# A spatial gate's mean taken by a centering product on TensorE, and a gelu with its addition folded in

## The chip, the cores and the metric

One core of one Trainium2 chip runs the kernel. The metric is the device time of one execution in microseconds (us), the median of the runs. The engines are TensorE (PE, its weight loads PEld), VectorE (DVE), ScalarE (ACT), GpSimd (POOL) and SyncE (SP), which issues the transfers.

## What is computed

One layer of a gated two-branch block on x (1024 tokens, width 1024), all in float32: a norm, one combined projection into nine parts, an attention branch (eight heads of 64), a spatial-gating branch, two merge gates, an output projection, a residual and a last norm. What the change touches is the spatial gate's v branch and the gelu in front of it:

```python
def spatial_gating(u, v, ln_g, ln_b, w_s, b_s):
    b, s, g, c = v.shape                       # 8 groups of 64 channels
    mu = jnp.mean(vf, axis=-1, keepdims=True)
    var = jnp.mean(jnp.square(vf - mu), axis=-1, keepdims=True)
    vn = (vf - mu) * lax.rsqrt(var + EPS) * ln_g + ln_b
    ...
    mixed = jnp.einsum('gts,bnsgc->bntgc', w, vn) + b_s ...
    return u * mixed

y_b = spatial_gating(jax.nn.gelu(u_b), jax.nn.gelu(v_b), ...) * jax.nn.silu(z_b)
```

The gelu is computed in its sigmoid form, v * sigmoid(1.5957691 * v * (1 + 0.044715 * v * v)).

## The kernel before

Every float32 product is made of three passes over operands that are split into a high and a low part (type fp32r): high by high, high by low, low by high. ScalarE casts the high part, VectorE or GpSimd subtracts it to get the low one (`hi_lo`, lines 214 to 216). The combined projection is done in groups of two 128-channel tiles by 1024 tokens; `project` (line 528) makes one group with seven products of twelve passes each (a Strassen scheme), and hands each finished 128 x 512 quarter to a function `use`. So each branch gets its data in quarters, channels on the partitions and tokens along the free axis.

No engine's order is written by hand. All operations are first recorded as tasks with an estimated cost (`Plan.add`, line 104); a list scheduler (`issue`, line 234) then plays them through on five engines and the transfer queue and issues them in the order that comes out. On each engine the ready task with the lowest priority number goes first. The number is the place in the program, less an offset: parts called through `ahead` (line 813) get 6000 off and the weights' preparation 9000, on every engine but TensorE. TensorE itself takes the earliest ready task of the program. A task starts only if its buffers are free, and buffers of one tag are granted in the order of the program: the tags "tr" and "z" have two PSUM banks each, "o", "X", "Y" and "Z" one, the small columns "s" sixteen buffers (line 353). At run time each engine works its list in order.

The sections come in this order (lines 827 to 854): the norm of x and the attention's values, then the first groups of keys and queries, u, the second gate path, v (`make_vb(0)`) and the attention's gate, the first attention head, then u, gate path and v of the second half (`make_vb(1)`) ahead of their turn, and the other heads with the remaining projections between them. In the trace the eight units of `make_vb` lie in 140 to 200 us and 250 to 306 us.

One unit of `make_vb` (lines 768 to 810) takes a quarter v, 128 channels (two groups of 64) by 512 tokens:

- `gelu_gate` (line 714): a square on ScalarE, an addition with a scale on ScalarE (`act_add`, line 149), a multiplication on VectorE, a sigmoid on ScalarE; then a multiplication by v.
- four transposes on TensorE into one "tr" bank (line 777), which put tokens on the partitions and channels along the free axis.
- a sum over each group's 64 channels (line 780), and the subtraction of sum / 64, out of PSUM into SBUF (line 781), both on VectorE.
- a square on ScalarE, a sum on VectorE, an addition and a power on GpSimd (`rms_scale`, line 395), a multiplication by the resulting scale on VectorE (line 787).
- the split into high and low parts, six passes with the spatial weights into "o", a copy by ScalarE, four transposes back into a "z" bank, scale and shift on VectorE, and a multiplication by u and the gate path on GpSimd, with a transfer in and one out.

The u branch uses `gelu_gate` too, in eight quarters.

Of the kernel before, what the change touches and what calls it, by code (L numbers as in the profile page):

```python
# [10 lines left out]
F32 = mybir.dt.float32  # L11
F32R = mybir.dt.float32r
AF = mybir.ActivationFunctionType
ALU = mybir.AluOpType
AX = mybir.AxisListType

P = 128
# [4 lines left out]
GELU_C = 0.044715  # L22
GELU_S = 1.5957691216057308
# [66 lines left out]
class Plan:  # L90
# [10 lines left out]
    def buf(self, tag, shape=(P, 512), dt=F32):  # L101
        return Buf(self, tag, shape, dt)
# [22 lines left out]


    def mm(self, out, lhsT, rhs, start, stop, **kw):
        self.add("PE", max(0.109, rhs.n * 0.000417 + 0.0135),
                 lambda: self.nc.tensor.matmul(out.ap(), lhsT=lhsT.ap(), rhs=rhs.ap(), start=start, stop=stop, **kw),  # L129
                 [out], [lhsT, rhs])  # L130

# [198 lines left out]
def hybrid_block(  # L330
# [15 lines left out]
    nc = tc.nc  # L346
# [3 lines left out]
    dram = ctx.enter_context(tc.tile_pool(name="dram", bufs=1, space=bass.MemoryType.DRAM))  # L350
    ps = ctx.enter_context(tc.tile_pool(name="ps", bufs=1, space=bass.MemoryType.PSUM))

    slots = {"T": 14, "k": 6, "r": 5, "ak": 4, "e": 4, "f1": 4, "f2": 6, "a": 7, "b": 8, "os": 2, "s": 16,
             "X": 1, "Y": 1, "Z": 1, "z": 2, "tr": 2, "o": 1}
    psum_tags = {"X", "Y", "Z", "z", "tr", "o"}
    uid = [0]
# [11 lines left out]
    pl = Plan(tc, make_tile, slots, psum_tags)  # L368
    buf = pl.buf

    def cbuf(shape):
        return buf("c", shape)

    ident = cbuf((P, P))
    make_identity(nc, ident.ap())
    ident = ident.all
    nhalf = cbuf((P, 16))
    nc.vector.memset(nhalf.ap(), -0.5)
    one = cbuf((P, 16))
    nc.vector.memset(one.ap(), 1.0)  # L380
    sums = cbuf((P, 16))
    gcol = cbuf((P, 16))
    shift = cbuf((P, 4, P))
# [2 lines left out]
    def small(c=1):  # L386
        return buf("s", (P, 16))[:, 0:c]

    def blocks(v, k):
        return v.map(lambda a: a.rearrange("p (k c) -> p k c", k=k))  # L390

    def half_of(half):
        return slice(half * 512, half * 512 + 512)

    def rms_scale(ss_in, cols):
        ms = small(cols)
        pl.ts(ms, ss_in, EPS, None, ALU.add, eng="POOL")
        r = small(cols)
        pl.rsqrt(r, ms, nhalf[:, 0:cols])
        return r  # L400
# [116 lines left out]
    T = {1: hq[0, 0], 2: hq[1, 0], 3: hq[1, 1]}  # L517
# [10 lines left out]
    def project(g, use, keep=True):  # L528

        use_at, pl.offset = pl.offset, -9000  # L530

        def after(j, half, v, in_psum):
            pl.offset = use_at
            use(j, half, v, in_psum)
            pl.offset = -9000

        raw = {}
        for q in ((0, 0), (1, 0), (1, 1), (0, 1)):
            raw[q] = buf("a", (P, 4, P))
            pl.load(raw[q].all, w_pairs[g, 2 * q[0] + q[1]].rearrange("p (k e) -> p k e", e=P))  # L540

        def parts(v, eng="DVE"):
            hi, lo = buf("b", (P, 4, P), F32R), buf("b", (P, 4, P), F32R)
            pl.hi_lo(hi.all, lo.all, v.all, eng)
            return hi, lo

        def product(i, w, acc, start, stop=True):
            n = 0
            for kt in range(4):
                for a, b in ((w[0], T[i][0]), (w[0], T[i][1]), (w[1], T[i][0])):  # L550
                    pl.mm(acc.all, a[:, kt, :], b[:, kt, :], start and n == 0, stop and n == 11,
                          skip_group_check=True)
                    n += 1

        groups[0] += 1
        y, z, xx = buf("XY"[groups[0] % 2]), buf("Z"), buf("YX"[groups[0] % 2])
        s1 = s2 = s4 = buf("a", (P, 4, P))
        w1 = parts(raw[0, 0])
        pl.tt(s1.all, raw[1, 0].all, raw[1, 1].all, ALU.add, eng="POOL")
        w5 = parts(s1)  # L560
        product(1, w1, y, True)
        pl.copy(xx.all, y.all)
        pl.tt(s2.all, s1.all, raw[0, 0].all, ALU.subtract)
        product(5, w5, z, True)
        p5 = buf("f2")
        pl.copy(p5.all, z.all)
        w6 = parts(s2)
        product(6, w6, y, False)
        u2 = buf("f2")
        pl.copy(u2.all, y.all)  # L570
        w2 = parts(raw[0, 1], "POOL")
        s3 = raw[1, 0]
        pl.tt(s3.all, raw[0, 0].all, raw[1, 0].all, ALU.subtract, eng="POOL")
        product(2, w2, xx, False)
        after(0, 0, xx.all, True)
        w7 = parts(s3)
        product(7, w7, y, False)
        pl.tt(p5.all, y.all, p5.all, ALU.add)
        after(1, 1, p5.all, False)
        pl.tt(s4.all, raw[0, 1].all, s2.all, ALU.subtract)  # L580
        w3 = parts(s4)
        product(3, w3, z, False)
        pl.tt(u2.all, z.all, u2.all, ALU.add)
        after(0, 1, u2.all, False)
        w4 = parts(raw[1, 1], "POOL")
        product(4, w4, y, False)
        if keep:
            c21 = buf("f2")
            pl.copy(c21.all, y.all)
            after(1, 0, c21.all, False)  # L590
        else:
            after(1, 0, y.all, True)
        pl.offset = use_at
# [4 lines left out]
    def near(in_psum):  # L598
        return "DVE" if in_psum else "POOL"
# [114 lines left out]
    def gelu_gate(v, tag="f1"):  # L714
        t = buf(tag)
        pl.act(t.all, v, AF.Square)
        pl.act_add(t.all, t.all, one[:, 0:1], GELU_C)
        pl.tt(t.all, t.all, v, ALU.mult)
        pl.act(t.all, t.all, AF.Sigmoid, scale=GELU_S)
        return t  # L720

    uz = [buf("d", (P, S)) for _ in range(4)]
# [10 lines left out]
    def make_zb(a):  # L733
        def use(j, half, v, in_psum):
            t = buf("f1")
            pl.act(t.all, v, AF.Sigmoid)
            pl.tt(t.all, t.all, v, ALU.mult, eng=near(in_psum))
            us = buf("f1")
            pl.load(us.all, u[2 * a + j][:, half_of(half)])
            pl.tt(us.all, us.all, t.all, ALU.mult, eng="POOL")  # L740
            pl.store(uz[2 * a + j][:, half_of(half)], us.all)
        project(ZB[a], use)

    def wide(v):
        return v.map(lambda a: a.unsqueeze(2).broadcast_to([P, 8, 64]))
# [19 lines left out]
    def make_vb(a):  # L765
        ws = {}

        def use(j, half, v, in_psum):
            e = 2 * a + j
            if j not in ws:  # L770
                ws[j] = mix_weights(e)
                make_shift(e, ws[j])
            t = gelu_gate(v, "r")
            pl.tt(t.all, t.all, v, ALU.mult, eng=near(in_psum))
            tr = buf("tr")
            for n in range(4):
                pl.transpose(tr[:, n * P:(n + 1) * P], t[:, n * P:(n + 1) * P], ident)
            t3 = blocks(t.all, 8)
            mu = small(8)
            pl.reduce(mu, blocks(tr.all, 8))  # L780
            pl.stt(t3, wide(mu), -1.0 / 64, blocks(tr.all, 8), ALU.mult, ALU.add)
            sq = buf("f1")
            pl.act(sq.all, t.all, AF.Square, scale=0.125)
            vs = small(8)
            pl.reduce(vs, blocks(sq.all, 8))
            r = rms_scale(vs, 8)
            pl.tt(t3, t3, wide(r), ALU.mult)
            hi, lo = buf("e", (P, 4, P), F32R), buf("e", (P, 4, P), F32R)
            pl.hi_lo(hi.all, lo.all, blocks(t.all, 4))

            mx = buf("ak", (P, 4, P))
            acc = buf("o")
            for gl in range(2):
                g = 2 * e + gl
                cs = slice(gl * 64, gl * 64 + 64)
                av = acc[:, gl * 256:gl * 256 + 256].map(lambda a: a.rearrange("p (n c) -> p n c", c=64))
                for n, (w, b) in enumerate(((0, hi), (0, lo), (1, hi))):
                    pl.mm(av, ws[j][:, 2 * w + gl, :], b[:, :, cs], gl == 0 and n == 0, gl == 1 and n == 2, skip_group_check=True)
            pl.copy(mx.all.map(lambda a: a.rearrange("p n (g c) -> p g n c", c=64)),
                    acc.all.map(lambda a: a.rearrange("p (g n c) -> p g n c", g=2, c=64)))  # L800
            tm = buf("z")
            for n in range(4):
                pl.transpose(tm[:, n * P:(n + 1) * P], mx[:, n, :], ident)
            m4 = mx.all
            pl.stt(m4, blocks(tm.all, 4), gcol[:, e:e + 1],
                   shift[:, e, :].map(lambda a: a.unsqueeze(1).broadcast_to([P, 4, P])), ALU.mult, ALU.add)
            us = buf("f1")
            pl.load(us.all, uz[e][:, half_of(half)])
            pl.tt(us.all, us.all, mx.all.map(lambda a: a.rearrange("p n c -> p (n c)")), ALU.mult, eng="POOL")
            pl.store(y_b[e][:, half_of(half)], us.all)  # L810
        project(VB[a], use)

    def ahead(fn, *args):
# [152 lines left out]
    for c in range(2):  # L966
        for a in range(2):
            t = buf("T", (P, 4, 512))
# [27 lines left out]
    for i in range(8):  # L996
# [7 lines left out]
        r = small()  # L1004
# [45 lines left out]
```

## Time and profile before

| | us |
|---|---|
| median of 3 runs | 766.98 (766.76 to 767.42) |
| the profiled execution | 766.53 |
| its span | 764.7 |
| TensorE busy | 735.0 |
| VectorE busy | 575.0 |
| ScalarE busy | 433.5 |
| GpSimd busy | 308.8 |

The profile is of one execution. Its span runs from the first instruction of the program to the last. Busy time is the union of an engine's instructions; matmuls overlap one another, so a mean length of one is longer than the distance between two. TensorE's granted clock is at the upper of its two levels, 2.4 GHz, but for a part of the last 25 us (0.96 on the mean there).

### The profile page before, as it was taken

Reading aid. Unit: us, or ns where it says so; the run is one execution under the profiler, and the core shown is the slowest. Engines: PE = TensorE matmul, PEld = TensorE weight load, DVE = VectorE, ACT = ScalarE, POOL = GpSimd, SP = SyncE. Lnnn points to the kernel's source line nnn. Section 1 sums busy time; section 2 is a strip of 40 time slices with the busy share of each in tenths; the row PEclk is TensorE's granted clock in tenths of the full one; section 3 lists DMA queues with packets and bytes.
Section 4 is the critical chain, followed back from the end, with each engine's and each line's share of the span. In section 5 each row is a group of like instructions: output and inputs, shape, how many; then the busy total and the mean of one; then the engine's idle time right before and its main releaser. Section 6 shows DMA issues by size and latency. Waiting matters only on the chain.

```text
span 764.7 us, 10791 instructions
## 1 busy us (share of the span) xinstructions
PE 735.0 (96%) x3524; PEld 606.4 (79%) x3524; DVE 575.0 (75%) x788; ACT 433.5 (57%) x920; POOL 308.8 (40%) x298
## 2 busy tenths in 40 slices
PE   4989999999889999999999999999999999999996
PEld 3877788888777888887888888878888887888885
DVE  4868754688899787898999988897998878841122
ACT  6636474756756755666757676676867433411122
POOL 1500637497666576274345538234140300013110
PEclk9999999999999999999999999999999999999999
DMA  9412494424344375454543656354597677760022
GB/s 338 176 64 96 144 255 159 146 96 138 113 127 127 103 212 185 141 166 137 153 124 114 191 165 180 108 137 127 173 311 255 213 237 231 252 228 1 29 82 111
DMA packets 69177, 121.31 MB, mean 159 GB/s; under 512 B 7296, under 2 KB 17024, under 8 KB 69120
## 3 DMA queue, kind: packets, MB, share of 16 engines
q1 hardware_dynamic: 67968, 118.52, 49.3%
q10 hardware_dynamic: 1152, 2.10, 0.7%
q8 instruction: 28, 0.46, 0.3%
q14 instruction: 29, 0.24, 0.1%
HBM read 81.27 MB, written 39.32 MB: 158 GB/s over the span
## 4 chain that ended last, share of the span: by engine, by line
PE 83%; DVE 9%; issue 3%; DMA 2%; ACT 2%; POOL 1%; SPq 0%; POOLq 0%; DVEq 0%; ACTq 0%
PE Y L129 22%; PE X L129 21%; PE Z L129 18%; PE z L129 9%; PE o L129 8%; PE tr L133 5%; DVE b L167 2%; DVE ak L198 1%; DVE ak L191 1%; DMA k<-in_x_dram 1%; DVE e L167 1%; DMA k<-d 1%; DVE T L167 1%; DVE f L167 1%; DVE r L167 1%
## 5 line engine op out<-in xcount | busy, mean ns | idle before, releaser
L129 PE MATMUL Y<-T,b 128*128 128x512 f32 x672 | 180.0, 398 | 1.6 <-ACT b L157 1.3
L129 PE MATMUL X<-T,b 128*128 128x512 f32 x660 | 177.9, 398 | 0.0
L129 PE MATMUL Z<-T,b 128*128 128x512 f32 x540 | 145.2, 397 | 0.0
L129 PEld LDWEIGHTS Y<-T,b 128*128 128x128 f32 x672 | 122.3, 188 | 26.0 <-ACT b L157 1.7
L157 ACT CAST b<-a 128x512 fp32r<-128x512 f32 (+1 forms) x152 | 93.6, 617 | 81.9 <-PE Y L129 22.5
L129 PEld LDWEIGHTS X<-T,b 128*128 128x128 f32 x660 | 119.8, 188 | 22.8 <-POOL b L167 0.4
L167 DVE TENSOR_TENSOR b<-a,b 128x512 fp32r<-128x512 f32 (+1 forms) x112 | 99.4, 889 | 28.8 <-ACT b L157 20.0
L129 PEld LDWEIGHTS Z<-T,b 128*128 128x128 f32 x540 | 98.1, 188 | 18.3
L167 POOL TENSOR_TENSOR b<-a,b 128x512 fp32r<-128x512 f32 x40 | 60.7, 1516 | 119.8 <-ACT b L157 106.6
L198 DVE TENSOR_TENSOR_SCAN ak<-ak,c 128x128 f32<-128x128 f32 (+1 forms) x64 | 72.8, 1141 | 3.5 <-ACT ak L146 3.4
L167 POOL TENSOR_TENSOR a<-a,a 128x512 f32<-128x512 f32 x40 | 61.5, 1537 | 28.9 <-DVE b L167 15.3
L167 POOL TENSOR_TENSOR f<-f,f 128x512 f32<-128x512 f32 (+1 forms) x38 | 56.2, 1484 | 36.0 <-ACT f L146 14.7
L157 ACT CAST e<-tr 128x512 fp32r<-128x512 f32 (+1 forms) x96 | 45.7, 480 | 36.5 <-PE tr L133 33.3
L167 POOL TENSOR_TENSOR r<-r,ak 128x512 f32<-128x512 f32 x32 | 46.9, 1474 | 39.4 <-DVE ak L191 33.4
L133 PE MATMUL tr<-c,r 128*128 128x128 f32 x320 | 58.5, 273 | 2.6 <-DVE r L167 2.5
L129 PE MATMUL o<-e,k 128*128 128x512 f32 (+1 forms) x192 | 57.6, 343 | 3.3 <-DVE e L167 3.2
L146 ACT ACTIVATE ak<-z 128x128 f32<-128x128 f32 (+2 forms) x96 | 47.4, 494 | 20.4 <-PE z L129 18.1
L129 PE MATMUL z<-k,k 128*128 128x512 f32 (+2 forms) x216 | 56.8, 352 | 0.9 <-DMA k<-d 0.9
L167 DVE TENSOR_TENSOR e<-tr,e 128x512 fp32r<-128x512 f32 (+1 forms) x96 | 52.0, 545 | 7.3 <-ACT e L157 6.4
L146 ACT ACTIVATE r<-z 128x128 f32<-128x128 f32 (+2 forms) x96 | 46.9, 495 | 13.1 <-PE tr L133 12.5
L133 PEld LDWEIGHTS tr<-c,r 128*128 128x128 f32 x320 | 39.9, 140 | 13.6 <-DVE r L167 3.4
L191 DVE TENSOR_TENSOR_SCAN ak<-ak,c 128x512 f32<-128x512 f32 x32 | 50.5, 1588 | 0.2
(217 smaller groups left out, 1148.5 us busy)
## 6 DMA issues: line engine op xcount, KB each, us to landing
d<-f SPq DMA_DIRECT2D x112, 256.0 KB, 2.8
a<-in_w_pairs_dram SPq DMA_DIRECT2D x80, 256.0 KB, 2.8
f<-d SPq DMA_DIRECT2D x72, 256.0 KB, 3.2
k<-d SPq DMA_DIRECT2D x48, 256.0 KB, 4.8
k<-in_x_dram SPq DMA_DIRECT2D x8, 512.0 KB, 7.2
d<-b SPq DMA_DIRECT2D x16, 256.0 KB, 2.3
k<-d SPq DMA_DIRECT2D x8, 512.0 KB, 6.3
a<-in_w_up_dram SPq DMA_DIRECT2D x16, 256.0 KB, 4.3
```

What stands on the lines that cost most here:

```text
L129: lambda: self.nc.tensor.matmul(out.ap(), lhsT=lhsT.ap(), rhs=rhs.ap(), start=start, stop=stop, **kw),
L133: self.add("PE", 0.109, lambda: self.nc.tensor.transpose(out=out.ap(), in_=in_.ap(), identity=ident.ap()), [out], [in_, ident])
L146: return self.nc.scalar.activation(out=out.ap(), in_=in_.ap(), func=func, scale=sc, **kw)
L157: lambda: self.nc.scalar.copy(out=out.ap(), in_=in_.ap()), [out], [in_])
L167: self.add(eng, cost, lambda: e.tensor_tensor(out=out.ap(), in0=in0.ap(), in1=in1.ap(), op=op), [out], [in0, in1])
L191: lambda: self.nc.vector.tensor_tensor_scan(out.ap(), in_.ap(), in_.ap(), 1.0 if init is None else init.ap(), op0=ALU.mult, op1=ALU.bypass),
L198: lambda: self.nc.vector.tensor_tensor_scan(out.ap(), in_.ap(), floor.ap(), init, op0=ALU.mult, op1=ALU.max), [out], [in_, floor])
```

## The change

The four transposes of a unit become four products of the same data with a constant matrix, the identity less 1/64 in each of its two 64 x 64 diagonal blocks. A product with the identity transposes; one with this matrix transposes and takes each group's mean off. The sum and the subtraction on VectorE go. The square reads the product's PSUM bank, and so does the multiplication by the scale, which before read what the subtraction had written to SBUF. The constant is made by three VectorE instructions ahead of the program. In the gelu, the addition on ScalarE and the multiplication on VectorE become one VectorE instruction, (v * v + 1 / 0.044715) * v, and the sigmoid's scale takes the factor. The scheduler's cost of a float32 product is doubled; there is no other product with a float32 moving operand. The "s" tag has eight buffers.

```diff
     def mm(self, out, lhsT, rhs, start, stop, **kw):
-        self.add("PE", max(0.109, rhs.n * 0.000417 + 0.0135),
+        self.add("PE", max(0.109, rhs.n * 0.000417 + 0.0135) * (2 if rhs.buf.dt == F32 else 1),
...
-    slots = {"T": 14, "k": 6, "r": 5, "ak": 4, "e": 4, "f1": 4, "f2": 6, "a": 7, "b": 8, "os": 2, "s": 16,
+    slots = {"T": 14, "k": 6, "r": 5, "ak": 4, "e": 4, "f1": 4, "f2": 6, "a": 7, "b": 8, "os": 2, "s": 8,
...
-    one = cbuf((P, 16))
-    nc.vector.memset(one.ap(), 1.0)
...
         pl.act(t.all, v, AF.Square)
-        pl.act_add(t.all, t.all, one[:, 0:1], GELU_C)
-        pl.tt(t.all, t.all, v, ALU.mult)
-        pl.act(t.all, t.all, AF.Sigmoid, scale=GELU_S)
+        pl.stt(t.all, t.all, 1.0 / GELU_C, v, ALU.add, ALU.mult)
+        pl.act(t.all, t.all, AF.Sigmoid, scale=GELU_S * GELU_C)
...
+    center = cbuf((P, P))
+    nc.vector.tensor_copy(center.ap(), ident.ap())
+    for gl in range(2):
+        cut = center.ap()[64 * gl:64 * gl + 64, 64 * gl:64 * gl + 64]
+        nc.vector.tensor_scalar(out=cut, in0=cut, scalar1=-1.0 / 64, scalar2=None, op0=ALU.add)
...
             for n in range(4):
-                pl.transpose(tr[:, n * P:(n + 1) * P], t[:, n * P:(n + 1) * P], ident)
+                pl.mm(tr[:, n * P:(n + 1) * P], t[:, n * P:(n + 1) * P], center.all, True, True)
             t3 = blocks(t.all, 8)
-            mu = small(8)
-            pl.reduce(mu, blocks(tr.all, 8))
-            pl.stt(t3, wide(mu), -1.0 / 64, blocks(tr.all, 8), ALU.mult, ALU.add)
             sq = buf("f1")
-            pl.act(sq.all, t.all, AF.Square, scale=0.125)
+            pl.act(sq.all, tr.all, AF.Square, scale=0.125)
             vs = small(8)
             pl.reduce(vs, blocks(sq.all, 8))
             r = rms_scale(vs, 8)
-            pl.tt(t3, t3, wide(r), ALU.mult)
+            pl.tt(t3, blocks(tr.all, 8), wide(r), ALU.mult)
```

## Rows read from the trace of the kernel before

**Rows 1.** The page: span, busy us (share of the span) and instructions by engine.

```profile
span 764.7 us, 10791 instructions
PE 735.0 (96%) x3524; PEld 606.4 (79%) x3524; DVE 575.0 (75%) x788; ACT 433.5 (57%) x920; POOL 308.8 (40%) x298
```

**Rows 2.** Stretches: length, busy of PE, PEld, DVE, ACT, POOL, clock, DMA share, GB/s.

```profile
140.00:200.00 60.00, 60.00 (x296) 50.19 (x295) 47.17 (x66) 39.83 (x72) 41.49 (x34) 1.00 0.35 115
200.00:240.00 40.00, 35.27 (x167) 28.00 (x167) 39.30 (x44) 26.44 (x63) 29.28 (x24) 1.00 0.39 123
240.00:310.00 70.00, 69.34 (x346) 57.45 (x345) 56.32 (x76) 41.30 (x79) 44.54 (x38) 1.00 0.54 163
310.00:650.00 340.00, 336.98 (x1663) 278.76 (x1661) 299.89 (x395) 218.12 (x497) 126.96 (x130) 1.00 0.57 175
```

**Rows 3.** TensorE's waits, 200 to 245 us: us in total, times, longest.

```profile
PE tr L133 <- DVE r L167: 2.5, 2, 1.5
PE o L129 <- DVE e L167: 2.4, 3, 1.5
```

**Rows 4.** Timeline of TensorE in the first units: start us, us, instructions.

```profile
152.80 0.60 PE L133 MATMUL tr<-c,r 128*128 128x128 f32 x4
...
154.40 2.89 PE L129 MATMUL Y<-T,b 128*128 128x512 f32 x12
...
158.04 0.60 PE L133 MATMUL tr<-c,r 128*128 128x128 f32 x4
```

**Rows 5.** VectorE's groups by form, 140 to 310 us: count, busy us, mean ns, idle before.

```profile
L167 DVE TENSOR_TENSOR r<-r,s 128x512 f32<-128x512 f32 x8 | 11.8, 1478 | 0.3 <-POOL s L167 0.2
...
L186 DVE TENSOR_REDUCE s<-tr 128x8 f32<-128x512 f32 x8 | 5.5, 686 | 1.2 <-PE tr L133 1.2
L173 DVE SCALAR_TENSOR_TENSOR r<-s,tr 128x512 f32<-128x512 f32 x8 | 5.5, 684 | 0.4
...
L167 DVE TENSOR_TENSOR r<-r,f 128x512 f32<-128x512 f32 x6 | 5.0, 841 | 0.9 <-ACT r L151 0.9
```

**Rows 6.** Groups by form: transposes and passes, ScalarE's additions, VectorE's multiply-add from SBUF.

```profile
L133 PE MATMUL tr<-c,r 128*128 128x128 f32 x16 | 2.4, 272 | 0.0
...
L129 PE MATMUL Y<-T,b 128*128 128x512 f32 x672 | 180.0, 398 | 1.6 <-ACT b L157 1.3
...
L173 DVE SCALAR_TENSOR_TENSOR k<-k,s,T 128x512 f32<-128x512 f32 x16 | 11.4, 746 | 5.3 <-DMA T<-in_norm_g_dram 4.8 <-POOL s L167 0.5
...
L151 ACT ACTIVATE f<-f,c 128x512 f32<-128x512 f32 x8 | 5.8, 728 | 0.2
...
L151 ACT ACTIVATE r<-r,c 128x512 f32<-128x512 f32 x8 | 5.8, 726 | 0.2
```

**Rows 7.** Timeline: the fourth unit's way to the first head, and a later unit's scaling.

```profile
181.73 0.67 DVE L186 TENSOR_REDUCE s<-f 128x8 f32<-128x512 f32 x1
...
188.00 1.79 DVE L167 TENSOR_TENSOR r<-r,s 128x512 f32<-128x512 f32 x1
...
198.01 0.60 PE L133 MATMUL z<-c,ak 128*128 128x128 f32 x4
...
198.36 0.42 PE L129 MATMUL z<-k,k 128*128 128x128 f32 x2
...
294.65 0.68 DVE L167 TENSOR_TENSOR r<-r,s 128x512 f32<-128x512 f32 x1
```

**Rows 8.** Timeline: VectorE ahead of the first norm, and small buffers in the last ones.

```profile
1.55 0.23 DVE L648 COPY c<-c 128x128 f32<-128x128 f32 x1
...
6.57 1.42 DVE L173 SCALAR_TENSOR_TENSOR k<-k,s,T 128x512 f32<-128x512 f32 x2 [4.79 <-DMA T<-in_norm_g_dram]
...
27.94 1.41 DVE L173 SCALAR_TENSOR_TENSOR k<-k,s,T 128x512 f32<-128x512 f32 x2
...
33.19 0.78 POOL L181 TENSOR_SCALAR s<-s 128x1 f32<-128x1 f32 x1
```

## The prediction

> **What bounds the kernel now.** I began with the busy times. The reader is to see in [rows 1] that TensorE is busy 735.0 of 764.7 us and VectorE 575.0: the first engine leaves only 29.7 us unused. A whole-span share says little of one stage, so the second view is the busy time by stretch [rows 2]. The spatial gate's eight units lie in 140 to 200 (the first four) and 240 to 310 (the other four). In the first of these TensorE is busy 60.00 of 60 us, in the second 69.34 of 70. Between them, in 200 to 240, the picture turns: VectorE works 39.30 of 40 us and TensorE idles 4.73. From 310 to 650 TensorE idles 3.0 of 340 us. So 4.7 + 0.7 + 3.0 = 8.4 us of idle lie in these stretches, and the other 21 us at the two ends of the program, where no unit of the gate runs. The third view, TensorE's waits, names what it waits for in 200 to 245: VectorE's results for the transposes and products of the first attention head, 2.5 + 2.4 us [rows 3]. What the change is worth is therefore read from TensorE alone: time that VectorE or ScalarE saves beside a busy TensorE is worth nothing, and each added TensorE nanosecond in 140 to 200 is paid in full.
>
> **The transposes become full products.** Eight units issue four each, 32 in all. As transposes, four take 0.60 us and the last one's own length is 0.272, so they start (0.60 - 0.272) / 3 = 0.109 us apart [rows 4, 6]. No row shows a float32 product that is not a transposition. Below, it costs as much as the transposition with the same operands: 0 added. Above, by rows: a single pass of fp32r operands over 512 columns takes (2.89 - 0.40) / 11 = 0.226 us [rows 4, 6], or 0.057 per 128 columns; a full-precision product could be four passes, at best 4 x 0.057 = 0.227 us, at worst four passes that each take a transposition's slot, 4 x 0.109 = 0.436. The change's own cost for its order of work says twice 0.109, 0.218. I take 0.218, since four bare passes come to nearly the same. Added: 32 x (0.218 - 0.109) = 3.5 us of TensorE, half of it in 140 to 200, where nothing can take it up. Ends for the range: 0 and 32 x 0.327 = 10.5 us.
>
> The Trainium skill speaks against this part: TensorE: Matmul & The Clock Gate, section Terms, says that the transpose mode is four times faster for float32. Read against the slot of 0.109 us it would make the product 0.436 us and the sum 10.5 instead of 3.5; read against a bare pass it agrees with what I took. No run here shows which.
>
> **VectorE loses work.** Per unit the first reduction (mean 686 ns) and the subtraction (684 ns) go [rows 5]: 8 x 1.37 = 11.0 us. The multiplication by the scale read two SBUF operands and took 1478 ns on the mean; it now reads the product's PSUM bank. The subtraction that is removed also read that bank and took 684 ns, so I take 0.69: 8 x 0.79 = 6.3 us more. The sixteen multiplications in the gelu change their form. The nearest rows of the new form are 746 ns from SBUF and 684 with one operand in PSUM, of the old form 841 ns on the mean in the second half of the units [rows 5, 6]: between 0.06 more and 0.1 less each, at most 1.6 us either way, which I put at nothing. So VectorE gives up some 17 us, all of it in 140 to 200 and 250 to 300, beside a TensorE that idles 0.0 and 0.7 us there. If that cover were gone, it would be worth the whole 17.
>
> **ScalarE loses the sixteen additions**, 8 x 0.728 + 8 x 0.726 = 11.6 us [rows 6], half of them in the u branch. ScalarE is busy 39.83 of 60 and 41.30 of 70 us in these stretches [rows 2]; TensorE covers it in the same way. What is queued behind them on ScalarE, the casts of weights that the next products need, comes earlier, but no TensorE wait in 140 to 310 is on a cast. The square now waits for TensorE's product and not for the subtraction behind it, which is earlier by 1.4 us of VectorE.
>
> **A wait moves.** The two PSUM banks "tr" were free after the subtraction; now a unit holds its bank until the scaled result is written. Before, that was the stretch from the second reduction to the end of the scaling, for the fourth unit 181.73 to 189.79, 8.1 us [rows 7]; with product and square in front, some 9 us. Units follow one another by 5.2 us (products at 152.80 and 158.04 [rows 4]), and with two banks the next but one must wait 9 us and has about 10. Behind a waiting product on TensorE stand the projections. I put it at nothing, and the bound is in the rivals.
>
> **Small edits.** The centering constant costs one copy and two short additions on VectorE ahead of the program; VectorE then sits idle 4.79 us for the norm's weights, and a copy of this size takes 0.23 [rows 8]: hidden; without the cover it is under 1 us. Eight instead of sixteen small buffers: at their tightest, in the first norm, the one taken by the addition at 33.19 would be the one last read by the multiplication that ended at 29.35 [rows 8]: 3.8 us to spare, so 0; with a queue at that place, under 1 us. No DMA is added, removed or moved past another by hand.
>
> **What comes back.** The first head's products start at 198.36, right behind the transposes of the fourth unit at 198.01 [rows 7]: both take the "z" banks in order. That unit's chain loses 1.37 us of reduction and subtraction and 1.79 - 0.69 = 1.1 us of scaling, so the head can start some 2.5 us earlier, in a stretch where VectorE has 12.8 of 60 us free: 2.5 x 12.8 / 60 = 0.5 us of the 4.7 is filled. Of the 0.7 us in 240 to 310 I take all. Late next, after both, is TensorE itself. Back: 1.2 us.
>
> **Sum.** 3.5 - 1.2 = +2.3 us against the profiled span of 764.7: 767.0. That execution took 766.5, so 1.9 lie around the span; the median of the runs shown, 766.98, stands 0.45 above it. Forecast: 766.98 + 2.3 = 769.3 us. A measurement of this kernel tells 0.2% (1.5 us) from no change.
>
> **Rivals.** *No change.* The order of work is drawn anew from about 100 us on, since sixteen additions and sixteen VectorE steps have other costs, and a lighter VectorE may remove 2 to 5 of the 8.4 us: 3.5 less 2 to 5 is within 1.5 of nothing, 765.5 to 768.5. For it: waits of 4.9 us on VectorE in one stretch where it is full [rows 2, 3]. Against it: none of the removed work lies in that stretch. 0.28.
>
> *Faster.* The head's earlier start spreads 39.3 us of VectorE work over a longer stretch and its waits vanish whole: 3.5 - 4.7 - 0.7 = -1.9, 765.1 us. It decides from 5 us recovered on, or from less if the product costs no more than a transposition (then -1.2 with my own 1.2, and over 0.2% from 1.5 recovered). 0.20.
>
> *The bank is held too long.* Units 3 and 4 of both groups wait on TensorE for their "tr" bank, with all projections behind them; if the scaling that frees it comes late by 1 us, as its length varies (0.68 to 1.79 [rows 7]), 4 x 1 = 4 us more, 773.3. Against it: the spacing just computed. 0.05.
>
> *The product takes four slots.* 10.5 - 1.2 = +9.3 us: 776.3 us. For it: the transposition's slot, nearly twice its bare pass, shows that a weight load costs something for each. Against it: weight loads run beside products everywhere else here. The sentence of the Trainium skill above (TensorE: Matmul & The Clock Gate, Terms) is this rule. 0.07.
>
> **How the numbers follow.** The forecast has 0.40. Slower takes the forecast and the last two rivals, 0.40 + 0.05 + 0.07 = 0.52; same 0.28; faster 0.20. The range goes from 764.5, under the faster case, to 775.0, over the held bank; it leaves out the four slots and the ends of the others, under 0.2.
>
> **What would show it.** Right: 32 products whose starts lie 0.22 us apart where the transposes were, TensorE's busy time up by 3 to 4 us, VectorE's down by about 17 and ScalarE's by about 12, and TensorE still busy through 140 to 200. Step by step: waits of TensorE on VectorE in 200 to 245 near 4 us. Wrong: those waits under 1 us (the faster case), a TensorE wait ahead of the centering products (the held bank), starts 0.4 us apart (four slots), or a TensorE that grows by nothing.

## The result, and the profile after

The changed kernel took 775.56 us (median of 4, 772.34 to 777.73) beside 767.2 before (766.76 to 767.75): a ratio of 1.0105, 95% interval 1.0069 to 1.0142, 8.4 us slower where 2.3 were forecast, and 0.6 us over the range.

The page of the changed kernel, its span and busy times, against [rows 1]:

```profile
span 774.2 us, 10824 instructions
PE 740.7 (96%) x3556; PEld 612.3 (79%) x3556; DVE 554.5 (72%) x774; ACT 421.3 (54%) x904; POOL 307.6 (40%) x298
```

The other engines lost somewhat more than the prediction said: VectorE 20.5 us, ScalarE 12.2. TensorE's busy time grew by 5.7 us, and of the 9.5 us by which this span is longer the other 3.8 are idle time. The 5.7 are not all work: 3.6 are the products (below), and the rest goes with two stretches at a lower granted clock, where before it was 1.00: 0.73 on the mean at 632 to 638 us (the last section has the line) and 0.72 here, ahead of every unit:

```profile
44.00:50.00 6.00, 6.00 (x25) 4.94 (x24) 4.00 (x10) 1.95 (x6) 0.00 (x0) 0.72 0.08 32
```

Where the idle time lies is in the busy times by stretch, first of the changed kernel, then of the one before for the two stretches that [rows 2] has not (columns as there):

```profile
140.00:200.00 60.00, 58.82 (x303) 49.16 (x302) 46.98 (x66) 36.96 (x77) 40.57 (x37) 1.00 0.37 120
200.00:240.00 40.00, 38.10 (x185) 30.70 (x184) 36.05 (x41) 24.22 (x52) 31.00 (x19) 1.00 0.44 136
240.00:310.00 70.00, 70.00 (x356) 59.03 (x355) 53.81 (x74) 42.68 (x89) 41.75 (x40) 1.00 0.50 159
310.00:590.00 280.00, 275.45 (x1367) 227.90 (x1366) 232.60 (x302) 184.34 (x419) 118.78 (x123) 1.00 0.52 161
590.00:665.00 75.00, 70.20 (x321) 57.70 (x321) 56.45 (x88) 31.23 (x67) 8.61 (x7) 0.98 0.68 216
```

```profile
310.00:590.00 280.00, 278.17 (x1386) 230.39 (x1385) 251.95 (x324) 194.12 (x446) 117.63 (x124) 1.00 0.54 164
590.00:665.00 75.00, 73.65 (x343) 60.67 (x343) 61.23 (x93) 31.94 (x65) 9.33 (x6) 1.00 0.72 237
```

Around the units, 140 to 310 us, TensorE idles 3.1 of 170 us where it idled 5.4: better by 2.3. From 310 to 665, where no instruction of the change lies, it idles 9.4 of 355 where it idled 3.2: worse by 6.2. The difference is the 3.8 us. TensorE's waits in that later part, us in total, times, longest, before and then after (the first line reads: TensorE, about to write tile Y, waited for VectorE to write tile T):

```profile
PE Y L129 <- DVE T L167: 1.3, 1, 1.3
PE z L129 <- DMA k<-d: 0.9, 2, 0.7
PE o L129 <- DVE e L167: 0.8, 1, 0.8
```

```profile
PE o L129 <- ACT e L157: 3.4, 1, 3.4
PE z L129 <- DMA k<-d: 3.4, 2, 2.3
PE Y L129 <- DVE T L167: 1.3, 1, 1.3
PE o L129 <- DVE e L167: 1.0, 2, 0.5
```

Two are new or longer: the last attention head waits for a cast, and the waits for the loads of keys grew from 0.9 to 3.4 us. The first is worth reading in the timeline of the changed kernel (start us, us, engine, line; in brackets the idle time before and what ended it):

```profile
619.21 0.38 SPq L230 DMA_DIRECT2D d<-f  x1
622.80 0.32 SPq L223 DMA_DIRECT2D f<-d  x1
...
624.16 1.43 SPq L223 DMA_DIRECT2D a<-in_w_out_dram  x3
...
627.75 0.60 PE L133 MATMUL tr<-c,r 128*128 128x128 f32 x4
...
630.64 0.62 ACT L157 CAST r<-a 128x512 fp32r<-128x512 f32 x1 [8.69 <-DMA a<-in_w_out_dram]
631.16 0.58 ACT L157 CAST e<-tr 128x512 fp32r<-128x512 f32 x1
...
631.79 0.80 PE L129 MATMUL o<-e,k 128*128 128x512 f32 x1 [3.45 <-ACT e L157]
632.38 1.48 PE L129 MATMUL Y<-T,b 128*128 128x512 f32 x3
```

Read it from below. TensorE waits 3.45 us for the cast of its own transposes, which were done at 628.35. ScalarE had nothing to do for 8.69 us, but the next instruction in its order was the cast of an output weight, and that weight's load was issued only at 624.16: SyncE stood from 619.6 to 622.8 in front of a load that needed a buffer back. From the issue to the cast went another 6.5 us. Three in-order queues stand behind one another. Three passes then take 1.48 us where [rows 4] has twelve in 2.89. In the profile before, the same loads went out at 614.90 and the cast ran at 619.75, 4.9 us later and ahead of need.

The products, in the timeline and as a group by form:

```profile
147.57 1.05 PE L129 MATMUL tr<-c,r 128*128 128x128 f32 x8
```

```profile
L129 PE MATMUL tr<-c,r 128*128 128x128 f32 x64 | 8.7, 274 | 0.0
```

Each of the 32 shows as two matmuls, 64 in all; eight start (1.05 - 0.275) / 7 = 0.111 us apart, so a product takes 0.22 us, as taken. In sum, start to start, they cost 32 x (0.221 - 0.109) = 3.6 us more than the transposes. (The expectations below reckon with 0.09 us for each; the trace gives 0.112.)

### The profile page after: what moved, and what is told of

Read it like the earlier page. It is cut to its first block, busy times and chain, and to the rows that moved or that the text cites. A ratio compares the mean times of both kernels' runs of the same rounds, so it can differ in the third digit from the quotient of the medians.

```text
span 774.2 us, 10824 instructions
## 1 busy us (share of the span) xinstructions
PE 740.7 (96%) x3556; PEld 612.3 (79%) x3556; DVE 554.5 (72%) x774; ACT 421.3 (54%) x904; POOL 307.6 (40%) x298
## 5 line engine op out<-in xcount | busy, mean ns | idle before, releaser
L129 PE MATMUL X<-T,b 128*128 128x512 f32 x660 | 176.0, 396 | 0.0
L129 PE MATMUL Z<-T,b 128*128 128x512 f32 x540 | 148.2, 399 | 0.0
L167 DVE TENSOR_TENSOR b<-a,b 128x512 fp32r<-128x512 f32 (+1 forms) x112 | 102.6, 918 | 35.3 <-ACT b L157 31.5
L167 POOL TENSOR_TENSOR b<-a,b 128x512 fp32r<-128x512 f32 x40 | 58.6, 1465 | 128.0 <-ACT b L157 118.7
L167 POOL TENSOR_TENSOR f<-f,f 128x512 f32<-128x512 f32 (+1 forms) x38 | 60.6, 1602 | 36.5 <-ACT f L157 13.5
L198 DVE TENSOR_TENSOR_SCAN ak<-ak,c 128x128 f32<-128x128 f32 (+1 forms) x64 | 68.9, 1078 | 3.5 <-ACT ak L146 3.3
L167 POOL TENSOR_TENSOR r<-r,ak 128x512 f32<-128x512 f32 x32 | 48.6, 1526 | 57.1 <-DVE ak L191 52.5
L129 PE MATMUL o<-e,k 128*128 128x512 f32 (+1 forms) x192 | 60.3, 347 | 4.9 <-ACT e L157 3.4
L133 PE MATMUL tr<-c,r 128*128 128x128 f32 x288 | 54.6, 274 | 2.7 <-DVE r L167 2.6
L129 PEld LDWEIGHTS z<-k,k 128*128 128x128 f32 x216 | 39.0, 188 | 11.1 <-issue 3.9
```

The source lines that it names most:

```text
L133: self.add("PE", 0.109, lambda: self.nc.tensor.transpose(out=out.ap(), in_=in_.ap(), identity=ident.ap()), [out], [in_, ident])
L167: self.add(eng, cost, lambda: e.tensor_tensor(out=out.ap(), in0=in0.ap(), in1=in1.ap(), op=op), [out], [in0, in1])
L198: lambda: self.nc.vector.tensor_tensor_scan(out.ap(), in_.ap(), floor.ap(), init, op0=ALU.mult, op1=ALU.max), [out], [in_, floor])
```

## The experiments

All ratios are to the kernel before on the same chip, with 95% intervals. The edits are abridged. The theory to test was that the products cost about 3 us and the rest comes from the order of work: the scheduler draws a new one whenever any cost changes. The rival was that all of it hangs on the products.

**Same order, transposes in place of the products.** In the changed kernel:

```diff
-pl.mm(tr[...], t[...], center.all, True, True)
+pl.add("PE", 0.218, lambda: nc.tensor.transpose(out=tr[...], in_=t[...], identity=ident), ...)
```

> The changed kernel with its order of work untouched, but each of the 32 centering products is a transposition again, planned at the product's cost. Left out: the group's mean is not taken off. Theory A (the change costs its products on TensorE, about 0.09 us each by the changed kernel's trace, and the rest of the 8.4 us is waits on transfers in the order of work that came out): TensorE busy falls by 3 us, the time to 772 or 773 us, 5 us above before. Theory B (all of the loss hangs on the products: their length, their banks held): back to 767 or 768 us.

772.66 us (770.0 to 775.79), 1.0094 (1.0057 to 1.0132): 3 us under the changed kernel by the medians, though the intervals of the two overlap. In the profiled execution, the fastest of the four (770.0), TensorE's busy time is 735.3, about that of before, and both waits are still there: 2.8 us on the cast, 2.5 on the loads of keys. Some 6 us stay with the products gone.

**Each half alone, order drawn anew.** The fold without the products, and the products with the old gelu:

```diff
 # the kernel before
-pl.act_add(t.all, t.all, one[:, 0:1], GELU_C)
-pl.tt(t.all, t.all, v, ALU.mult)
+pl.stt(t.all, t.all, 1.0 / GELU_C, v, ALU.add, ALU.mult)
```

> The kernel before with the gelu's addition folded in and nothing else; the scheduler draws a new order of work, TensorE's work is the same 735 us. Theory A: off from before by what other waits the new order brings, over 1.5 us in one direction or the other, with TensorE waits on transfers or casts that before did not have. Theory B: 767 us within 1 us, since ScalarE's 11.6 us lie beside a busy TensorE.

777.73 us, 1.0146 (1.0125 to 1.0167). Half of the change, with less work on ScalarE and no more on TensorE, loses as much as the whole or more (the intervals overlap). Its waits from 310 to 665 us:

```profile
PE o L129 <- ACT e L157: 3.5, 1, 3.5
PE z L129 <- DMA k<-d: 3.2, 2, 2.0
```

They are those of the changed kernel. It was not expected that they come back at the same places.

> The changed kernel with the old gelu (addition on ScalarE, multiplication on VectorE); the products stay. Theory A: 767 + 3 us of products + other waits than the changed kernel's, since the order is drawn anew: 769 to 777 us, with the waits at other places. Theory B: the same 775 us as the whole change, with the time lost where the units are (140 to 310 us).

This run also has seven small buffers and not eight. 781.0 us, 1.0189 (1.0152 to 1.0226), above the span of either theory, with a wait of 2.8 us on the same cast and 2.1 on the loads of keys. The halves' losses, 1.5 and 1.9%, do not add to that of the whole, as costs of operations would.

**The output weights' loads issued by ScalarE**, order untouched:

```diff
-pl.load(raw.all, w_out[kt, :, c * 512:c * 512 + 512])
+pl.load(raw.all, w_out[kt, :, c * 512:c * 512 + 512], nc.scalar)
```

> The changed kernel with the order of work on every engine untouched, but the sixteen loads of the output weights are issued by ScalarE and not by SyncE. Theory A: in the changed kernel the last attention head's products waited 3.45 us at 628 us for a cast on ScalarE that stood behind the cast of an output weight whose load SyncE had issued late, behind loads that waited for buffers; issued by ScalarE the load comes early, the wait at 628 us and the half-clock matmuls behind it go: 5 us less, 770 to 771 us. Theory B: no difference, 775 us.

775.88 us, 1.0119 (1.0087 to 1.0151): nothing gained, a miss. The wait at 628 us is gone, but TensorE idled later:

```profile
655.03 0.50 PE L129 MATMUL Y<-T,T 128*128 128x512 f32 x1 [0.96 <-ACT T L157]
...
657.63 0.80 PE L129 MATMUL X<-T,T 128*128 128x512 f32 x1 [1.17 <-DVE f L167]
659.56 1.65 PE L129 MATMUL Y<-T,T 128*128 128x512 f32 x3 [1.14 <-DVE T L167]
```

SyncE's waits for a buffer whose store had to finish, from 590 to 665 us, grew; before, the changed kernel, this run:

```profile
SPq L223 <- DMA d<-f: 18.7, 11, 3.2
```

```profile
SPq L223 <- DMA d<-f: 32.8, 13, 4.6
```

```profile
SPq L223 <- DMA d<-f: 39.0, 13, 4.7
```

That they are what costs the time is not shown: the order with loads planned longer, below, has as much of them at 769.55 us.

```profile
SPq L223 <- DMA d<-f: 33.9, 12, 4.8
```

**The order of before, kept.** These two decide. The scheduler plans the old costs, so each engine's order stays, and only what is issued differs:

```diff
 # products: a full product with the identity, planned at a transposition's cost
-pl.transpose(tr[...], t[...], ident)
+pl.add("PE", 0.109, lambda: nc.tensor.matmul(tr[...], lhsT=t[...], rhs=ident, start=True, stop=True), ...)
```

> The kernel before, with its order of work kept on every engine, but the 32 transposes of the gate's units are full products with the identity (the same result). Theory A (order): only the products' own price, 32 x 0.09 = 2.9 us, 769 to 770 us; no wait of TensorE on a cast at 620 to 635 us. Theory B (products): most of the 8.4 us, 774 to 775 us, since the product's length moves everything behind it.

771.71 us, 1.0054 (1.0038 to 1.0070): 2.9 to 5.4 us for the products in the order of before, against 3.6 by the trace; the median is over the 769 to 770 of theory A and under the 774 of B. No wait on the cast at 620 to 635 us; two waits of some 1.3 us stand at 652 to 656 us, one of them in the kernel before as well.

```diff
 # fold: the addition's time stays planned, but nothing is issued for it
-pl.act_add(t.all, t.all, one[:, 0:1], GELU_C)
-pl.tt(t.all, t.all, v, ALU.mult)
+pl.add("ACT", cost_of_act_add, lambda: None, ...)
+pl.add("DVE", cost_of_tt, lambda: nc.vector.scalar_tensor_tensor(...), ...)
```

> The kernel before, with its order of work kept on every engine, but the gelu's addition is folded in: the sixteen additions on ScalarE are not issued though the scheduler still plans their time. Theory A: 766 to 767 us, where the same fold with a newly drawn order took 777.7; what that run lost is the order alone. Theory C (the fold itself is slow, by the multiply-add on VectorE or its wait): 773 to 778 us here too.

766.19 us, 0.9986 (0.9970 to 1.0003): no difference, against 777.73 for the same operations in the new order. The fold is not slow; its order was. ScalarE's 11 us were worth nothing, as forecast.

**No operation changed, order drawn anew.** One number of the scheduler, its allowance for a hand-over between engines:

```diff
-LAT = 0.7
+LAT = 0.69
```

> The kernel before with no operation changed: the scheduler's allowance for a hand-over between engines is 0.69 us and not 0.70, which draws another order; its own estimate of the length moves by 0.1 us (758.0 to 758.2). Theory A: 770 to 780 us, as for the fold alone, with waits on transfers at 510 us and on a cast behind an output weight at 625 us. Theory B: 767 us within 1 us.

775.75 us, 1.0102 (1.0071 to 1.0132). A kernel with the operations of before loses as much as the whole change. Its span and busy times, and its waits from 310 to 665 us:

```profile
span 775.3 us, 10795 instructions
PE 737.3 (95%) x3524; PEld 608.8 (79%) x3524; DVE 565.6 (73%) x788; ACT 432.6 (56%) x920; POOL 308.8 (40%) x298
```

```profile
PE z L129 <- DMA k<-d: 4.7, 4, 2.4
PE o L129 <- ACT e L157: 4.2, 1, 4.2
```

And in its timeline the same queue as in the changed kernel:

```profile
630.61 0.62 ACT L157 CAST r<-a 128x512 fp32r<-128x512 f32 x1 [9.50 <-DMA a<-in_w_out_dram]
631.13 0.58 ACT L157 CAST e<-tr 128x512 fp32r<-128x512 f32 x1
```

The changed kernel and the fold alone with 0.60, and the kernel before with 0.60:

> The changed kernel with no operation changed: the allowance for a hand-over is 0.60 us and not 0.70, which draws another order; the scheduler's own estimate is 758.2 us and not 761.7. Theory A: off from 775.6 by more than 2 us in either direction (768 to 782), since the waits lie elsewhere. Theory B: 775 us within 1.5 us.

> The gelu's fold alone, allowance 0.60 us; the transposes stay. The scheduler's estimate is 754.7. Theory A: TensorE's work is that of before, so 764 to 770 us, where the same fold at 0.70 took 777.7. Theory C (the fold is slow of itself): 775 us or more.

> The kernel before with the allowance for a hand-over at 0.60 us, as in the run of the changed kernel that took 770.9; no operation changed. Theory A: anything from 764 to 774; the change at this allowance then costs the products' 3 to 4 us with the rest of either sign. Theory B: 767 us, and the change at this allowance 4 us.

770.9 us (1.0046, 1.0025 to 1.0067), 772.12 (1.0080, 1.0056 to 1.0103) and 775.55 (1.0118, 1.0094 to 1.0141). The fold is outside both of its theories. At this allowance the changed kernel is the fastest of the three by the medians (its interval overlaps the fold's, not that of the operations of before). A comparison of two orders tells nothing of the operations until the spread of orders is known.

**The output weights' casts planned later**, by their landing time alone:

```diff
 pl.load(raw.all, w_out[kt, :, c * 512:c * 512 + 512])
+pl.tasks[-1].tail = 6.0
```

> The changed kernel; the scheduler believes that a load of the output weights takes 6 us to land and not 2, so ScalarE's casts of these weights stand behind the last head's casts. The order is the same on every engine up to there (some 615 us). Theory A: the wait of 3.45 us at 628 us and the half clock behind it go; 770 to 772 us. Theory A2 (the stretch from 590 to 660 us is paced by the transfers of the other branch's merged products, and the wait was only where it showed): the time stays at 774 to 776 us, with new waits at 640 to 665 us, as when ScalarE issued these loads.

773.23 us (770.39 to 774.49), 1.0090 (1.0073 to 1.0107). In its trace, of the fastest of four executions (770.39), the wait at 628 us is gone; the median gives back 2.3 of the 5 us hoped for, and the intervals overlap. Neither A nor A2 is met. So the wait that shows best is not the whole loss: with it gone, one run gained nothing and this one 2.3 us.

**Every load planned with 3.5 us to land** and not 2.0. The plan adds this to a load's own time in its queue, 0.75 us for 256 KB, so it believed in 2.75 us and now in 4.25; in the profile before, the medians of 256 KB loads from issue to landing are 2.8 to 6.7 us by kind. The edit:

```diff
 def load(...):
-                 tail=2.0)
+                 tail=3.5)
```

> The changed kernel; the scheduler believes that every load takes 3.5 us to land and not 2.0 (the trace has 2.7 to 7 by kind). Its own estimate is the same, 761.8. Theory A: waits of TensorE on loads and on casts of loads fall from 7 us to under 3; 769 to 772 us. If the order alone is a lottery that this does not touch: 770 to 778 us.

769.55 us (768.62 to 769.87), 1.0033 (1.0020 to 1.0046), the steadiest of the new orders. Its waits from 310 to 665 us:

```profile
PE Y L129 <- ACT T L157: 2.2, 1, 2.2
PE o L129 <- DVE e L167: 0.5, 1, 0.5
PE z L129 <- DMA k<-d: 0.5, 1, 0.5
```

The waits on the keys' loads are 0.5 us in place of 3.4, and that on the cast is gone. The same planning for the operations of before, at both allowances, and for the fold alone:

> The kernel before, no operation changed, every load planned with 3.5 us to land and not 2.0; a newly drawn order. If the too short landing time is why new orders lose time (theory A3), 765 to 769 us although the scheduler's own estimate rises from 758.0 to 762.2. If new orders lose time whatever the landing time (theory A, a lottery of which before holds a good ticket): 770 to 777 us, as the other two new orders of these operations (775.8 and 775.6).

> The kernel before with the allowance for a hand-over at 0.69 us, as in the run that took 775.8 with no operation changed, and every load planned with 3.5 us to land. Theory A3: 765 to 769 us, most of the 8.7 us gone. Theory A: 770 to 777 us.

> The gelu's fold alone with every load planned with 3.5 us to land; transposes stay, TensorE's work is that of before. Theory A3: 765 to 767.5 us, 2 to 3 us under the whole change in this planning (769.6), which would be at or under before. Theory A: 770 to 777 us (777.7 in the planning of before).

771.99 us (1.0057, 1.0039 to 1.0075), 768.28 (1.0017, 1.0008 to 1.0027) and 766.56 (0.9995, 0.9981 to 1.0008). Where the planning with 2.0 us had given 775.75 and 777.73, this one gives 768.28 and 766.56, and for the whole change 769.55 in place of 775.56: three orders gain 6 to 11 us. The order of before, at 767 a good one, loses 5 by it. The four orders planned so took 766.6 to 772.0 us, eight orders planned with 2.0 us 767 to 781. That speaks for the short landing time as a cause, but does not show it: the operations of before at the old allowance missed the 765 to 769 us that this theory asked for and came out where the rival, a lottery of orders, has them, and another allowance alone had brought the changed kernel from 775.56 to 770.9. No version here is clear of the kernel before on the fast side.

## Why the prediction was wrong

**The bound** was read rightly. TensorE sets the time: 11 us of ScalarE's work gone from the same order moved nothing.

**The products** (3.5 us forecast): 3.6 us by the trace, 0.22 us for one as taken, and 2.9 to 5.4 us as an experiment in the order of before. This term was right, and the rival of four slots, 0.436 us each, is out. The sentence of the Trainium skill weighed there (TensorE: Matmul & The Clock Gate, Terms), that the transpose mode is four times faster for float32, does not hold here when it is read against the transposition's slot: 0.221 us against 0.109 is two times.

**VectorE and ScalarE** (17 and 11.6 us): 20.5 and 12.2 of busy time, nearly all beside a busy TensorE. The scaling out of PSUM takes 686 ns, as the removed subtraction did:

```profile
L167 DVE TENSOR_TENSOR r<-tr,s 128x512 f32<-128x512 f32 x8 | 5.5, 686 | 2.7 <-POOL s L167 2.6
```

**The bank** put at nothing cost nothing: no TensorE wait stands ahead of a centering product in the changed kernel's trace.

**What comes back** (1.2 us): too little. The head starts not 2.5 but 17 us earlier, at 180.98 against 198.36 [rows 7], again right behind the fourth unit's transposes:

```profile
180.62 0.60 PE L133 MATMUL z<-c,ak 128*128 128x128 f32 x4
180.98 0.42 PE L129 MATMUL z<-k,k 128*128 128x128 f32 x2
```

Of these 17 us, 2.5 are the work taken off the chain; the rest came with the new order. 2.3 us came back between 140 and 310.

**The step that failed** is the term for the order of work. The sum has none, which puts it at nothing; the rival "no change" said that the order is drawn anew, and counted that as something that could only remove idle time: "2 to 5 of the 8.4 us". The 3.2 us of idle in 310 to 665 were taken as a cost to be lowered, not as a good result that the new order could lose. The runs showed 6.2 us more idle there and slower passes behind the longest wait. The term that was missing, a new order's own loss, has a size of 0 to 11 us: the operations of before in four other orders took 768.3 to 775.8, and the fold alone, worth nothing in the order of before, 777.7 in a new one. That is larger than any term in the sum, and the evidence was in the rows: TensorE busy 99% from 310 to 650 beside a VectorE at 88% leaves an order little to win and much to lose. Which waits of a bad order make up its loss stays open.

The forecast of 2.3 us stands near what the change costs where the order is planned with the longer landing time, 769.55 us. That is one order of several, and no confirmation of the sum.

## What to carry to other kernels

Where a list scheduler writes the order, a changed cost is a changed order everywhere behind it. Price an edit twice: its operations, with the order held (plan the old costs, issue the new work), and the spread of orders, by a few runs in which nothing but a scheduler's constant moves. Before that, look at what the plan believes of transfers: here it took 2.75 us for loads that land in 2.8 to 6.7, and the longest wait stood where a cast of a load was put in front of urgent work on an in-order engine. Taking that one wait away gave back 0 and 2.3 us, so measure again before calling it the cause.

## What was not expected of the hardware

A float32 product of 128 x 128 x 128 shows as two matmuls, each as long as a transposition's slot: 0.111 us each against 0.109.

One wait of TensorE cost more than its length. In the changed kernel it waited 3.45 us at 628 us; the stretch behind it has a granted clock of 0.73 on the mean, a part of it at the lower level of 1.2 GHz, and seven passes stand 0.43 us apart where 0.23 is usual:

```profile
626.00:632.00 6.00, 2.55 (x15) 1.95 (x14) 0.26 (x2) 1.36 (x3) 0.00 (x0) 0.98 0.88 276
632.00:638.00 6.00, 6.00 (x20) 4.83 (x21) 3.74 (x7) 1.89 (x4) 0.00 (x0) 0.73 0.62 212
638.00:644.00 6.00, 6.00 (x28) 4.95 (x28) 5.29 (x8) 2.96 (x5) 1.80 (x1) 1.00 0.77 256
```

Twenty matmuls in the six us behind the wait, 28 in the six after: over 1 us on top of the 3.45. Behind the 4.2 us wait of the kernel before at an allowance of 0.69 it is the same, with 16 matmuls:

```profile
632.00:638.00 6.00, 6.00 (x16) 4.66 (x17) 3.52 (x6) 1.52 (x4) 0.00 (x0) 0.54 0.70 244
```

Not every wait is followed by it: behind the changed kernel's 2.3 us wait for keys at 517 us the granted clock stayed at 1.00.

The new orders are also less steady: executions of the changed kernel differ by 5.4 us, those of before on the same chip by 1.0 (though on another chip one of 27 took 771.8). In part this goes with the granted clock. The changed kernel's span is 770.5 us in the execution with a mean clock of 0.997 and 773.4 to 776.0 in the three with 0.994; with transposes in place of its products it is 768.2 and 768.5 at 0.998, 773.0 and 774.0 at 0.994. With the products in the order of before it does not: 769.4 and 769.7 at 0.993, 770.1 to 771.7 at 0.996. Loads that land late could stand behind it too, but the orders with the longer landing time spread over 1.3 us (five executions) in one case and 4.2 (ten) in another, and no run isolates it.
